# SwiGLU-like gate on one core: load 2 held until tile 1 has landed, the last tile in parts of 2, 3 and 3 rows, one closing wait instruction

## The chip, the core and the metric

The kernel runs on one core of a Trainium2 chip. A core has a matrix engine (TensorE, unused here), VectorE (DVE), ScalarE (ACT), GpSimd (POOL) and SyncE (SP), and 16 DMA engines that move data between the device's memory (HBM) and the on-chip memory (SBUF, 128 partitions). Two instruction streams issue DMAs in this kernel, SP and ACT; each fills a queue of its own (q1 for SP, q10 for ACT in the profile), and both queues are served by the same 16 DMA engines.

The metric is device time in microseconds of one execution. Before the change the median of three runs is 471.4 us (471.35 to 471.65).

## The reference

The input x has 32 x 512 rows of 2048 float32 values. The left half of each row goes through SiLU and is multiplied with the right half; the result has 1024 float32 values a row.

```python
half_dim = x.shape[-1] // 2
x1, x2 = (x[..., :half_dim].copy(), x[..., half_dim:].copy())
silu_x1 = x1 * (1 / (1 + np.exp(-x1)))
return (silu_x1 * x2).astype(np.float32)
```

134.22 MB are read and 67.11 MB written; there is one SiLU and one product per output value.

## The kernel before

The 16384 rows are cut into 16 tiles of 128 partitions x 8 rows (K = 8). A whole tile is 8.4 MB in and 4.2 MB out. In a whole load, each of the 128 partitions takes 8 consecutive rows, which lie together in HBM, so a partition's share is one contiguous piece of 64 KB; its share of a whole store is one piece of 32 KB. There are two input buffers (xt0, xt1) and two output buffers (ot0, ot1), used in turn, and SiLU is written in place into the left half of the input buffer.

The order of the work on each engine is the order in which the program writes it (`tc.manual_schedule()`); an instruction waits for what it reads, and for the readers of what it overwrites.

- Tiles 0 and 1 are loaded in halves of 4 rows, one half by SP and one by ACT (`load_rows`, lines 53 to 54 and 71 to 73). The pieces of these four loads are 32 KB. All four are issued at the start.
- Tile 0 is computed in four parts of 2 rows (`FIRST`), each one SiLU (`silu`, line 58, ScalarE) and one product (`mul`, line 62, VectorE). It is stored by three DMAs from ACT, over every second partition and two sets of every fourth (`OPENING`, line 81). Then SP issues the load of tile 2 (`load(2)`, line 82, which runs line 51). That load overwrites xt0, so it waits for the last product of tile 0.
- For tiles 1 to 14 there is one SiLU, one product, one store from ACT (`store`, line 67) and, up to tile 13, one load of tile i + 2 from SP (line 51). The product waits for the SiLU, and for the store of tile i - 2 to have left its output buffer. The load waits for the product.
- The last tile, 15, is computed in the parts of `LAST`: two of 4 rows. Both SiLUs and products are written first, then the stores (`store`, line 67), so on ScalarE both SiLUs stand ahead of the first store's issue.
- At the end SP gets two empty instructions (`nc.sync.nop()`, line 100). The first waits for the eleven DMAs before the last one, the last SiLU and the last product; the second waits for the last store. After them the program's own end (line 128) waits for what is still open and synchronizes all engines.

`dmas` is the list of all DMAs in the order in which they are written: entries 0 and 1 are the halves of tile 0, entries 2 and 3 those of tile 1, then come the three stores of tile 0, and then load 2.

Of the kernel before, what the change touches and what calls it, by code (L numbers as in the profile page):

```python
# [1 line left out]

# [4 lines left out]


K = 8

FIRST = [(0, 2), (2, 4), (4, 6), (6, 8)]

LAST = [(0, 4), (4, 8)]


OPENING = [slice(0, None, 2), slice(1, None, 4), slice(3, None, 4)]
SYNC = mybir.DependencyInfo(mybir.DependencyClass.Sync, mybir.DependencyReason.DATA)


@with_exitstack  # L20
def kernel(
    ctx: ExitStack,
    tc: tile.TileContext,
    x: bass.AP,
    out: bass.AP,
):
    nc = tc.nc
    P = nc.NUM_PARTITIONS

    x_flat = x.flatten_outer_dims()  # L30
    out_flat = out.flatten_outer_dims()
    num_rows, in_cols = x_flat.shape
    half = in_cols // 2
    dt = x_flat.dtype
    n_tiles = num_rows // (P * K)
    assert n_tiles * P * K == num_rows

    x_view = x_flat.rearrange("(n p k) d -> n p k d", p=P, k=K)
    out_view = out_flat.rearrange("(n p k) d -> n p k d", p=P, k=K)

    in_pool = ctx.enter_context(tc.tile_pool(name="in_pool", bufs=1))
    out_pool = ctx.enter_context(tc.tile_pool(name="out_pool", bufs=1))
    xts = [in_pool.tile([P, K, in_cols], dt, name=f"xt{j}") for j in range(2)]
    ots = [out_pool.tile([P, K, half], dt, name=f"ot{j}") for j in range(2)]

    ctx.enter_context(tc.manual_schedule())

    dmas = []

    def load(i):  # L50
        dmas.append(nc.sync.dma_start(out=xts[i % 2], in_=x_view[i]))

    def load_rows(queue, i, a, b):
        dmas.append(queue.dma_start(out=xts[i][:, a:b], in_=x_view[i][:, a:b]))  # L54

    def silu(i, a, b):
        x1 = xts[i % 2][:, a:b, :half]
        return nc.scalar.activation(out=x1, in_=x1, func=mybir.ActivationFunctionType.Silu)  # L58

    def mul(i, a, b):  # L60
        xt = xts[i % 2]
        return nc.vector.tensor_mul(  # L62
            out=ots[i % 2][:, a:b], in0=xt[:, a:b, :half], in1=xt[:, a:b, half:]
        )

    def store(i, a, b):
        dmas.append(nc.scalar.dma_start(out=out_view[i][:, a:b], in_=ots[i % 2][:, a:b]))

    for i in range(2):
        load_rows(nc.sync, i, 0, K // 2)
        load_rows(nc.scalar, i, K // 2, K)

    for i in range(n_tiles - 1):
        if i == 0:
            for a, b in FIRST:
                silu(0, a, b)
                mul(0, a, b)
            for ps in OPENING:  # L80
                dmas.append(nc.scalar.dma_start(out=out_view[0][ps], in_=ots[0][ps]))
            load(2)
            continue
        silu(i, 0, K)
        mul(i, 0, K)
        store(i, 0, K)
        if i + 2 < n_tiles:
            load(i + 2)

    i = n_tiles - 1  # L90
    for a, b in LAST:
        last_silu = silu(i, a, b)
        last_mul = mul(i, a, b)
    for a, b in LAST:
        store(i, a, b)

    for waited in ([*dmas[-12:-1], last_silu, last_mul], dmas[-1:]):
        seen = nc.sync.nop()  # L100
        for ins in waited:
            tc.add_manual_dep(seen.ins, ins.ins.name, SYNC, reason="the closing waits")


# [1 line left out]
_INS = ['x']  # L106
_OUTS = [((32, 512, 1024), 'float32')]


# [23 lines left out]
```

## Time and profile before

| what | value |
|---|---|
| median of three runs | 471.4 us |
| profiled execution, its own time | 471.62 us |
| its span, first to last instruction | 469.7 us |
| VectorE busy | 139.4 us (30%), 20 products |
| ScalarE busy | 114.1 us (24%), 20 SiLUs and one table load |
| queue q1 (SP: all whole loads, a half of tiles 0 and 1) | 125.83 MB, 62.2% of the DMA engines' time |
| queue q10 (ACT: all stores, a half of tiles 0 and 1) | 75.50 MB, 37.2% |
| HBM read and written | 134.22 MB and 67.11 MB, 429 GB/s over the span |
| whole load, from issue to landing | 42.0 us (median of 14) |
| whole store, from issue to landing | 49.1 us (median of 14) |
| SiLU and product of a whole tile | 7.03 us and 8.69 us |

How to read it: a queue's share is the time that its packets took on the 16 engines, so the two shares together tell how full the DMA engines were. The time from issue to landing includes the time that a DMA's pieces stand behind others on their queue. Each DMA leaves, on every engine that it uses, its data pieces and one short write that reports completion; in the profile these short writes are the packets under 512 B. A window of the DMA view puts a piece's bytes and time into the slice in which the piece starts; where slices are shorter than a piece, the digits show starts, and zeros between them are no idleness by themselves. "Idle before" is what an engine waited for ahead of a group of instructions.

### The profile page before, as it was taken

The page shows a single profiled execution, that of the slowest core. Times are in us where ns is not written, and L with a number is a line of the kernel's source. Part 1 is how long each engine was busy: PE and PEld are TensorE (multiplying, and loading weights), DVE is VectorE, ACT ScalarE, POOL GpSimd, SP SyncE. Part 2 cuts the span into 40 slices and gives each one's busy share as a digit, 9 for nine tenths or more (in the row PEclk, how much of TensorE's full clock was granted, in tenths as well). Part 3 has the DMA queues.
Part 4 walks back from the last instruction along what each step waited for, and adds up shares of the span by engine and source line. Part 5 has one row for each costly group of instructions (what it writes and reads, how often), then busy time and mean ns, then how long its engine had stood idle before and what let it go on. Part 6 is the DMA issues. An engine that isn't in the chain of part 4 may idle for free.

```text
span 469.7 us, 199 instructions
## 1 busy us (share of the span) xinstructions
DVE 139.4 (30%) x20; ACT 114.1 (24%) x21; POOL 0.2 (0%) x4
## 2 busy tenths in 40 slices
DVE  0070704207042070510606115060250702407061
ACT  1053205050140501405023050230503205032060
POOL 0000000000000000000000000000000000000000
DMA  8999998999999999999999999999999899999998
GB/s 357 441 424 430 402 480 374 441 491 402 446 402 486 407 402 446 463 430 402 444 419 477 402 438 410 446 446 421 427 491 435 368 446 491 402 447 402 438 410 357
DMA packets 5073, 201.34 MB, mean 429 GB/s; under 512 B 592, under 2 KB 592, under 8 KB 592
## 3 DMA queue, kind: packets, MB, share of 16 engines
q1 hardware_dynamic: 2304, 125.83, 62.2%
q10 hardware_dynamic: 2768, 75.50, 37.2%
q14 instruction: 1, 0.01, 0.0%
HBM read 134.22 MB, written 67.11 MB: 429 GB/s over the span
## 4 chain that ended last, share of the span: by engine, by line
DMA 80%; DVE 14%; ACT 2%; DVEq 1%; issue 0%; ACTq 0%
DMA out_dram<-ot 62%; DMA xt<-in_x_dram 18%; DVE ot L62 14%; ACT xt L58 2%; DVEq L128 1%; DVEq L62 0%; ACTq L54 0%; ACTq L58 0%
## 5 line engine op out<-in xcount | busy, mean ns | idle before, releaser
L62 DVE TENSOR_TENSOR ot<-xt 128x8192 f32<-128x8192 f32 (+2 forms) x20 | 139.4, 6984 | 320.1 <-ACT xt L58 177.3
L58 ACT ACTIVATE xt<-xt 128x8192 f32<-128x8192 f32 (+2 forms) x20 | 112.8, 5661 | 338.4 <-DMA xt<-in_x_dram 338.4
L58 ACT ACT_TABLE_LOAD x1 | 1.3, 1283 | 1.6 <-PEq L117 1.6
L117 POOL MEMSET const-bfloat16-1.0<- 128x1 bf16 x1 | 0.1, 101 | 0.0
L117 POOL MEMSET const-uint8-127<- 128x1 uint8 x1 | 0.1, 101 | 0.0
L117 POOL MEMSET const-float32-0.0<- 128x1 f32 x1 | 0.1, 98 | 0.2 <-issue 0.2
L117 POOL MEMSET const-float32-1.0<- 128x1 f32 x1 | 0.1, 98 | 0.0
## 6 DMA issues: line engine op xcount, KB each, us to landing
out_dram<-ot ACTq DMA_DIRECT2D x14, 4096.0 KB, 49.1
xt<-in_x_dram ACTq DMA_DIRECT2D x2, 4096.0 KB, 31.7
xt<-in_x_dram SPq DMA_DIRECT2D x2, 4096.0 KB, 31.5
out_dram<-ot ACTq DMA_DIRECT2D x3, 2048.0 KB, 9.2
out_dram<-ot ACTq DMA_DIRECT2D x2, 1024.0 KB, 38.7
xt<-in_x_dram SPq DMA_DIRECT2D x14, 42.0
```

The costliest lines, as they stand in the source:

```text
L58: return nc.scalar.activation(out=x1, in_=x1, func=mybir.ActivationFunctionType.Silu)
L62: return nc.vector.tensor_mul(out=ots[i % 2][:, a:b], in0=xt[:, a:b, :half], in1=xt[:, a:b, half:])
L117: nc = _bacc.Bacc("TRN2", target_bir_lowering=False, num_devices=1)
L128: with _tile.TileContext(nc) as tc:
```

## The change

There are three edits.

1. Load 2 gets two further dependencies: on the two half-loads of tile 1 (`dmas[2:4]`). It is issued only when both have landed, and as before only after the last product of tile 0.
2. `LAST` becomes three parts of 2, 3 and 3 rows. The last tile so has three SiLUs, three products and three stores; as before, all SiLUs and products are written ahead of the stores.
3. One empty SyncE instruction instead of two. It waits for the eleven DMAs before the last one and for the last product. The last SiLU is no longer named (the last product reads its result), and the last store is left to the program's own end.

```diff
-LAST = [(0, 4), (4, 8)]
+LAST = [(0, 2), (2, 5), (5, 8)]
...
-        return nc.scalar.activation(out=x1, in_=x1, func=mybir.ActivationFunctionType.Silu)
+        nc.scalar.activation(out=x1, in_=x1, func=mybir.ActivationFunctionType.Silu)
...
             load(2)
+            for ins in dmas[2:4]:
+                tc.add_manual_dep(dmas[-1].ins, ins.ins.name, SYNC, reason="behind tile 1")
             continue
...
     for a, b in LAST:
-        last_silu = silu(i, a, b)
+        silu(i, a, b)
         last_mul = mul(i, a, b)
     for a, b in LAST:
         store(i, a, b)
...
-    for waited in ([*dmas[-12:-1], last_silu, last_mul], dmas[-1:]):
-        seen = nc.sync.nop()
-        for ins in waited:
-            tc.add_manual_dep(seen.ins, ins.ins.name, SYNC, reason="the closing waits")
+    seen = nc.sync.nop()
+    for ins in [*dmas[-12:-1], last_mul]:
+        tc.add_manual_dep(seen.ins, ins.ins.name, SYNC, reason="the closing waits")
```

## The prediction

> **What bounds the kernel now.** I read the page first, then the table of stretches, then DMA packets in short windows, then the chain of waits and the timeline at both ends.
>
> ```profile
> DVE 139.4 (30%) x20; ACT 114.1 (24%) x21; POOL 0.2 (0%) x4
> q1 hardware_dynamic: 2304, 125.83, 62.2%
> q10 hardware_dynamic: 2768, 75.50, 37.2%
> DMA 80%; DVE 14%; ACT 2%; DVEq 1%; issue 0%; ACTq 0%
> ```
>
> The two DMA queues (q1 is filled by SP, q10 by ACT) hold the 16 DMA engines for 62.2 + 37.2 = 99.4% of the span; VectorE and ScalarE are far from full. The stretches (columns: us, length, VectorE, ScalarE and GpSimd busy, clock, DMA share, GB/s) say where anything is lost:
>
> ```profile
> 22.00:41.00 19.00, 8.90 (x4) 7.31 (x4) 0.00 (x0) 1.00 0.99 426
> 41.00:70.00 29.00, 8.69 (x1) 7.10 (x2) 0.00 (x0) 1.00 1.00 416
> 70.00:99.00 29.00, 8.69 (x1) 7.13 (x2) 0.00 (x0) 1.00 1.00 434
> 446.00:458.00 12.00, 7.29 (x2) 7.12 (x2) 0.00 (x0) 1.00 0.98 423
> 458.00:467.00 9.00, 1.47 (x1) 0.00 (x0) 0.00 (x0) 1.00 1.02 435
> 467.00:469.70 2.70, 0.00 (x0) 0.00 (x0) 0.00 (x0) 1.00 0.24 103
> ```
>
> 434 GB/s is the full rate. The tail keeps it with q10 alone; the last piece ends at 468.36 in the DMA records, 1.3 us before the end. Only 41 to 70, where load 2 starts, runs below the steady rate. A closer window, first at 41:45, then the same place one tile later at 70:74 (40 slices of 0.1 us; a digit stands where pieces start):
>
> ```profile
> DMA  9999999900000000000000000000000000007999
> ```
> ```profile
> DMA  9999990000000000000000007999770000000999
> ```
>
> Pieces of load 2 start at 41.1 to 41.8 and the next pieces only from 44.6: 3.5 us. One tile later a load piece is followed after 2.4 us. In the DMA records the first piece of load 2 takes 3.4 to 3.7 us on all 16 engines, every later load piece 2.418: a stall of 1.09 us per engine. Counted by bytes, 41:70 moved 12.06 MB against 12.58 in 99:128: 0.52 MB, 1.2 us at 434 GB/s. So in the middle there is one stall of about 1.1 us to win and nothing else.
>
> ```profile
> DMA packets 320, 12.06 MB, mean 416 GB/s; under 512 B 80, under 2 KB 80, under 8 KB 80
> ...
> DMA packets 288, 12.58 MB, mean 434 GB/s; under 512 B 32, under 2 KB 32, under 8 KB 32
> ```
>
> The second line also gives the rhythm: 288 packets in 29 us are 128 load pieces of 64 KB, 128 store pieces of 32 KB and 32 completion writes, so per engine 9 turns of q1 and 9 of q10, one against one.
>
> **The change part by part.** (1) Load 2 waits for tile 1. In the chain of waits and the timeline:
>
> ```profile
> 1.17 41.16 DMA xt<-in_x_dram
> 404.83 42.15 DMA xt<-in_x_dram
> 455.13 4.34 DVEq L128
> ```
> ```profile
> 33.64 24.82 SPq L51 DMA_DIRECT2D xt<-in_x_dram  x2
> 33.64 1.84 ACTq L81 DMA_DIRECT2D out_dram<-ot  x3
> 42.35 7.03 ACT L58 ACTIVATE xt<-xt 128x8192 f32<-128x8192 f32 x1 [12.27 <-DMA xt<-in_x_dram]
> ```
>
> Tile 1 lands at 1.17 + 41.16 = 42.33; the issue of load 2 moves from 33.64 to about 42.4. On SP only load 3 stands behind it, and that waits for the product of tile 1 until 58.1, so nothing else is held; POOL issues nothing. From issue to first piece the only row without a backlog is the start: issue at 0.73, first pieces 1.73 to 2.5, so 1.0 to 1.8 us. Load 2's pieces start at 43.4 to 44.2 instead of 41.1. The engines don't idle meanwhile: the three stores of tile 0 (8 pieces per engine, 9.8 us) were issued at 33.64 and stand on q10. They get 2 or 3 turns alone (1.22 us each), and all loads come that much later, all stores sooner. Loads have room: load i+2 is issued 16 us after load i lands, load i+1 ends 29 us after it, so q1 doesn't run dry; nor does q10, since store 1 comes at 58.1 and store 0 lasts beyond 65. Products that now wait for a store (142.8 us in the waits, with Silu ending within 0.1 us of the landing) will wait for Silu instead.
>
> What becomes of the stall is the one large unknown. Bounds: it goes (-1.09), it stays with the first store piece (0), it comes twice (+1.09). Nearest rows: at 21.7 to 22.4 both queues pass to the next DMA at once without a stall (the next pieces follow at the usual pitch), and at 448.4 q10 alone passes from one store to the next without one; at 69 and 98 a load's first piece stands behind a store piece, and is not late. After the change load 2's first piece stands behind store pieces, as in those rows; I take -1.09. Against it: the turn from loads alone to stores happens nowhere else, so those rows can't exclude that it is the store's own start that stalls.
>
> (2) The last tile. At the last load's completion write an engine has 2 pieces of store 13 and 8 of store 14 before it: 10 x 1.22 = 12.2 us, which is 446.0 to 458.2. With 2 or 3 turns given away at the start, store 13 is done and 8 pieces remain (the third turn is a completion write): 9.8 us. By then the first store of the last tile must have come. Rows of the shapes:
>
> ```profile
> L62 DVE TENSOR_TENSOR ot<-xt 128x2048 f32<-128x2048 f32 x4 | 8.9, 2287 | 24.7 <-ACT xt L58 24.7
> L62 DVE TENSOR_TENSOR ot<-xt 128x4096 f32<-128x4096 f32 x2 | 8.8, 4422 | 16.6 <-ACT xt L58 16.6
> L58 ACT ACTIVATE xt<-xt 128x2048 f32<-128x2048 f32 x4 | 7.3, 1897 | 19.8 <-DMA xt<-in_x_dram 19.8
> L58 ACT ACTIVATE xt<-xt 128x4096 f32<-128x4096 f32 x2 | 7.1, 3608 | 21.8 <-DMA xt<-in_x_dram 21.8
> ```
>
> Two Silus take 7.1 us, four take 7.3, so three 7.2. The stores stand behind them on ScalarE: the first issues 0.1 + 7.2 = 7.3 us after the landing (before: 455.16 - 446.98 = 8.2), its product long done (1.9 + 2.3 = 4.2). With 1.0 to 1.8 to the first piece that is 8.3 to 9.1. The cover of 9.8 counts from the completion write, up to 0.5 before the landing on the engine that is last, 1.1 on the first: it ends 8.7 to 9.3 after the landing. So a gap of 0 to 0.4, or none on the late engines; I take +0.15. The last product ends at 1.9 + 2.3 + 3.35 x 2 = 10.9 after the landing instead of 459.5 - 446.98 = 12.5; two stores of work cover that. Smaller pieces: 64, 32 and 16 KB take 2.418, 1.213 and 0.611 us, so each has a fixed 8 ns; 24 instead of 16 pieces per engine cost 0.065.
>
> (3) Closing. The last landing is at 459.50 + 9.2 = 468.7, the end at 469.70. After the landing SP passes steps of about 0.07 us. One empty instruction fewer may remove one or two, and the last store's wait falls to the program's own end: -0.15 to +0.15, taken as -0.05.
>
> Sum: -1.09 + 0.15 + 0.065 - 0.05 = -0.93. The profiled execution took 471.62 (span 469.70, 1.92 around it) and would take 470.7; it lies 0.22 above the median of 471.4, so 470.5 against that median. 0.2%, 0.94 us, is about what a measurement of this kernel can tell from no change: the forecast lies on that edge.
>
> **The rivals.** (a) The stall stays, carried by the first store piece. Then 2 turns at most are given away, no gap comes, and the sum is 0.065 - 0.05: 471.4. For it: the turn from loads to stores has its only row at 41. (b) Slower: the load gives away too many turns. Place: the first store of the last tile. From the fourth turn on each takes 1.22 us of the cover. At four the gap is 0.2 to 1.0, at five 1.4 to 2.2, and 470.5 becomes 472.2; with the stall kept, 473. It decides where the issue of a DMA beside busy queues takes 3 us or more to its first piece. Against it: the 1.0 to 1.8 of the start; for it: no row shows a first piece beside a busy other queue. (c) Pieces are not shared one by one when a queue joins late: load 2 waits for all 8 store pieces, to 51, which takes 8 more turns or 9.8 us from the cover; the tail opens by some 9 us: 479. Against it: the 66.7 to 33.5% shares of q1 and q10 in 99:128 and the one-for-one order at 41. The Trainium skill (DMA: Bandwidth & Descriptors, Queues, rings and completion order) says that an engine drains some 9 to 17 descriptors of one row before it passes to the next, which would be this case; the trace's order of one piece each disagrees.
>
> **How the numbers follow.** Stall gone, tail covered: 0.48, 470.2 to 471.0, six tenths of it beyond 0.2%. (a) 0.35, 471.2 to 471.7, nearly all within 0.2%. (b) 0.15, up to 473, most of it slower. (c) 0.02. The likeliest gives 470.5; the range from 470.1 to 472.2 leaves out the ends of (b), (c) and a little below. Faster 0.48 x 0.6 = 0.29; slower 0.13 of (b), 0.02 of (c), 0.02 of (a) = 0.17; the rest 0.54 is the same.
>
> **What would show it.** Load 2's issue at 42.4 and its first pieces at 43.4 to 45; in 41:45 store pieces every 1.22 us; 41:70 at 434 GB/s. The last load landing 1 to 3 us later than 446.98; the first store of the last tile issued 7.3 us after that, and 434 GB/s from there to the end. Wrong would be: a hole after 41 (a), a hole some 10 us after the last landing (b), load 2's pieces starting only at 51 (c).

## The result and the profile after

The changed kernel takes 472.42 us (median of 17 runs, 472.02 to 472.86) against 471.51 us before (median of 17, 471.05 to 472.44). The ratio is 1.002, with a 95% interval of 1.0012 to 1.0027: 0.9 us slower, where 0.9 us faster was forecast. The profiled execution took 472.85 us; its span is 470.7 us against 469.7.

The page of the changed kernel (busy time, the two queues with their packets, MB and share, and the chain that ended last):

```profile
DVE 139.5 (30%) x21; ACT 114.2 (24%) x22; POOL 0.2 (0%) x4
q1 hardware_dynamic: 2304, 125.83, 62.0%
q10 hardware_dynamic: 2912, 75.50, 37.3%
DMA 72%; DVE 14%; ACT 11%; DVEq 1%; issue 0%; ACTq 0%
```

The bytes are the same and the engines are as busy as before; ScalarE's share of the chain rose from 2% to 11%, because the products on the chain now wait for their SiLU and no longer for a store. The table of stretches of the changed kernel (us, length, VectorE, ScalarE and GpSimd busy, clock, DMA share, GB/s) says where the time went:

```profile
41.00:70.00 29.00, 8.69 (x1) 7.03 (x1) 0.00 (x0) 1.00 0.99 425
70.00:99.00 29.00, 8.69 (x1) 7.03 (x1) 0.00 (x0) 1.00 1.00 434
...
446.00:458.00 12.00, 2.54 (x2) 4.84 (x3) 0.00 (x0) 1.00 0.97 418
458.00:460.80 2.80, 2.80 (x1) 2.38 (x1) 0.00 (x0) 1.00 0.90 375
460.80:462.00 1.20, 1.20 (x2) 0.00 (x0) 0.00 (x0) 1.00 0.14 58
462.00:469.00 7.00, 2.38 (x1) 0.00 (x0) 0.00 (x0) 1.00 1.02 428
```

From 70 on the middle runs at the full 434 GB/s. New is the row 460.80 to 462.00: 58 GB/s, while VectorE is busy all the time. Summed over the DMA records, the 16 engines stand idle there for 1.1 us on average. Before, that part of the tail was full. The timeline of the changed kernel, at the front and in the last tile, and the end of its chain of waits:

```profile
33.65 1.83 ACTq L81 DMA_DIRECT2D out_dram<-ot  x3
43.47 7.03 ACT L58 ACTIVATE xt<-xt 128x8192 f32<-128x8192 f32 x1 [13.38 <-DMA xt<-in_x_dram]
43.61 15.98 SPq L51 DMA_DIRECT2D xt<-in_x_dram  x2
...
453.16 4.56 ACT L58 ACTIVATE xt<-xt 128x2048 f32<-128x2048 f32 x2 [22.09 <-DMA xt<-in_x_dram]
455.10 2.29 DVE L62 TENSOR_TENSOR ot<-xt 128x2048 f32<-128x2048 f32 x1 [15.31 <-ACT xt L58]
457.43 0.34 ACTq L67 DMA_DIRECT2D out_dram<-ot  x1
457.63 2.75 ACT L58 ACTIVATE xt<-xt 128x3072 f32<-128x3072 f32 x1
457.75 6.63 DVE L62 TENSOR_TENSOR ot<-xt 128x3072 f32<-128x3072 f32 x2 [0.36 <-ACT xt L58]
461.15 3.60 ACTq L67 DMA_DIRECT2D out_dram<-ot  x2
```
```profile
410.47 42.60 DMA xt<-in_x_dram
453.08 0.02 issue
453.10 0.02 ACTq L58
453.11 0.04 issue
453.16 4.57 ACT xt L58 x2
457.73 0.02 issue
457.75 3.36 DVE ot L62
461.11 3.27 DVEq L130
```

The last load lands at 453.08 instead of 446.98, 6.1 us later. Its first store is issued at 457.43, and its pieces follow store 14 at 458.3 with hardly a gap. They are 8 pieces of 8 KB per engine, 2.5 us, and on most engines done near 460.85. The second product can't start before the second SiLU ends at 457.7; it ends at 461.11, its store is issued at 461.15, and the first pieces start at 461.99. That is the hole.

The spans add up. The last piece ends at 469.57 instead of 468.36, 1.21 us later; from there to the end of the span it is 1.16 us instead of 1.34. Together 1.0 us.

At the front, the DMA view of the changed kernel, 41:45 in slices of 0.1 us and 43:51 in slices of 0.2 (a digit stands where pieces start):

```profile
DMA  0000008000007999700700007999900700007999
```
```profile
DMA  0099730099703099703099907099700009907079
```

From 42.2 on store pieces start every 1.22 us, as expected. But load 2, issued at 43.6, has its first piece only at 47.2 to 48.6, by engine, after four or five store pieces: 3.6 to 5.0 us after the issue. (The expectations below were written with 6.2 as the upper end; counted by the first piece of each engine it is 5.0.) The engines don't lose the same number of turns, and the last load's reports of completion arrive from 450.0 to 453.1, by engine, where before they arrived from 446.3 to 447.0.

### The profile page after: what moved, and what is told of

The parts are those of the page before. It is cut to its first block, busy times and chain, and to the rows that moved or that the text cites. A ratio compares the mean times of both kernels' runs of the same rounds, so it can differ in the third digit from the quotient of the medians.

```text
span 470.7 us, 202 instructions
## 1 busy us (share of the span) xinstructions
DVE 139.5 (30%) x21; ACT 114.2 (24%) x22; POOL 0.2 (0%) x4
## 4 chain that ended last, share of the span: by engine, by line
DMA 72%; DVE 14%; ACT 11%; DVEq 1%; issue 0%; ACTq 0%
DMA xt<-in_x_dram 72%; DVE ot L62 14%; ACT xt L58 11%; DVEq L130 1%; ACTq L54 0%; ACTq L58 0%
```

## The experiments

Each experiment has its own runs of the kernel before beside it, with medians of 471.44 to 471.51 (the ratios and 95% intervals are those on record; they can differ from the quotient of the two medians by 0.05%). The theory (T) after the result: the wait lets q10 run ahead, which takes away the backlog of stores that covered the computation of the last tile, and the loss is the hole there. The rivals: the loss is made at the front (F), by the small parts (P), or by the closing (C).

### The wait alone

```diff
             load(2)
+            for ins in dmas[2:4]:
+                tc.add_manual_dep(dmas[-1].ins, ins.ins.name, SYNC, reason="behind tile 1")
```

> Load 2 waits for tile 1; the last tile stays in two parts of 4 rows and the closing waits stay as before. Theory T (the loss is a hole in the DMA stream of the last tile, because the wait takes the store backlog away that covered its SiLU and product): the last load lands near 453.1 as in the changed kernel, the first product ends 8.1 us later at 461.2, its first store pieces start near 462.0, store 14 ends near 458.4, so a hole of 3.5 to 3.7 us and about 475.1 us, slower than the changed kernel itself. Rival F (the loss is made at the front, by the later start of load 2 and the engines that fall out of step, and the parts of the last tile do not matter): the same 472.4 as the changed kernel.

475.54 us, ratio 1.0081 (1.0067 to 1.0094): 4.0 us slower than before, and 3.1 slower than the whole change. The stretches of its tail:

```profile
446.00:458.00 12.00, 1.56 (x1) 5.21 (x2) 0.00 (x0) 1.00 0.95 410
458.00:458.90 0.90, 0.90 (x1) 0.90 (x1) 0.00 (x0) 1.00 0.01 0
458.90:461.70 2.80, 2.80 (x2) 1.01 (x1) 0.00 (x0) 1.00 0.00 0
461.70:471.00 9.30, 3.50 (x1) 0.00 (x0) 0.00 (x0) 1.00 1.03 435
```

No data piece starts from about 458 to 461.7. The last load landed at 452.71, the first product of 4 rows was ready at 460.9, its pieces start at 461.74. Theory T holds in place and size: the records have 3.5 us of idle time per engine here, of the 4.0 that were lost. F falls as the main cause of this loss, since the same front gives another time with other parts; some 0.5 us are left for it.

### The parts alone

```diff
-LAST = [(0, 4), (4, 8)]
+LAST = [(0, 2), (2, 5), (5, 8)]
```

> Only the parts of the last tile become 2, 3 and 3 rows. Theory T: the last load lands near 447.0 as before, store 14 lasts to 458.2, the stores of the last tile are issued at 451.3, 455.0 and 458.3, each before its turn, so no hole; 8 more pieces per engine at 8 ns cost 0.065: 471.6 against 471.5 before. Rival P (the smaller parts themselves lose the time, because the first store is too short to cover the second product): slower by 0.9, 472.4.

471.77 us, ratio 1.0001 (0.9993 to 1.001): the same as before. In the last tile the DMA stream has no hole:

```profile
446.00:458.00 12.00, 8.47 (x3) 7.22 (x3) 0.00 (x0) 1.00 0.97 416
458.00:460.80 2.80, 0.36 (x1) 0.00 (x0) 0.00 (x0) 1.00 1.03 436
460.80:462.00 1.20, 0.00 (x0) 0.00 (x0) 0.00 (x0) 1.00 1.01 430
```

The small first store costs nothing while the backlog lasts to 458 and the second store is issued at 455.1. P falls.

### The closing alone

```diff
-    for waited in ([*dmas[-12:-1], last_silu, last_mul], dmas[-1:]):
-        seen = nc.sync.nop()
...
+    seen = nc.sync.nop()
+    for ins in [*dmas[-12:-1], last_mul]:
...
```

> Only the closing waits become one empty instruction. In the changed kernel the end comes 0.78 us after the last landing (469.92 to 470.70), before it came 0.97 after it (468.73 to 469.70). Theory T: 0.1 to 0.2 us faster than before, 471.3. Rival C (the closing holds the loss): slower by about 0.9.

471.30 us, ratio 0.9992 (0.9983 to 1.0002). The interval holds both no change and 0.2% less; slower by 0.9 us is out, so C falls. That it gains 0.1 to 0.2 us is likely and not shown by the times. In the traces, one execution each, the end of the span comes 0.82 us after the last landing, against 0.97 before.

### The whole change with four parts of 2 rows

```diff
-LAST = [(0, 2), (2, 5), (5, 8)]
+LAST = [(0, 2), (2, 4), (4, 6), (6, 8)]
```

(against the changed kernel)

> The changed kernel with the last tile in four parts of 2 rows. The last landing stays near 453.1. Theory T: products end 4.3, 6.5, 8.7 and 10.9 us after the landing, each store is 2.5 us of pieces from 458.4 on (to 460.9, 463.4, 465.9, 468.4), and the second store is issued near 459.6 with its first pieces near 460.5, before 460.9: no hole, and 471.3 to 471.5, within 0.2 of before. Rival F: the loss stays, 472.4.

472.10 us, ratio 1.0012 (1.0004 to 1.0021). The hole is gone:

```profile
458.00:460.80 2.80, 2.80 (x2) 2.25 (x2) 0.00 (x0) 1.00 0.92 386
460.80:462.00 1.20, 1.20 (x2) 0.00 (x0) 0.00 (x0) 1.00 1.04 437
```

The second product ends at 459.4 here, in time. Yet only 0.3 us of the median and 0.7 of the span are won back, not 0.9 to 1.1: the time is still 0.6 above before, which is what rival F asks of a part of the loss. One reason is in the DMA records of the changed kernel: the hole of 1.1 is a mean. In that execution the slowest engine ends its pieces of the first store at 462.07, when the second store's pieces are there, and hardly waits at all: without the hole it would have ended no sooner. In the other profiled execution of the changed kernel (next section) the slowest engine is done at 461.15 and waits 0.8 us. So what the hole costs depends on how late the slowest engine of an execution is; by the medians, 472.10 against 472.42, it is 0.3 us.

### The changed kernel again, and the four parts without the wait

The first of these two is the changed kernel itself, measured again beside the four-part kernel without the wait, on another chip than the experiments above.

> The changed kernel beside the others of this call on the same chip, so that hole, parts and wait are compared under like conditions. Expected 472.4; the hole of about 1.1 us in 460 to 462 of its DMA stream again.

472.54 us, ratio 1.0022 (1.0014 to 1.0031), and 1.07 us of idle time between 460 and 462. Against this median the four parts are worth 0.4 us.

Four parts and the single closing instruction, without the wait:

```diff
-LAST = [(0, 4), (4, 8)]
+LAST = [(0, 2), (2, 4), (4, 6), (6, 8)]
...
-    for waited in ([*dmas[-12:-1], last_silu, last_mul], dmas[-1:]):
-        seen = nc.sync.nop()
...
+    seen = nc.sync.nop()
+    for ins in [*dmas[-12:-1], last_mul]:
...
```

(against the kernel before)

> The kernel with the wait ended at 472.1 with four parts of 2 rows and no hole, still about 0.6 above before. This one has the same four parts and the same single closing instruction, but load 2 does not wait. Theory W (what is left of the loss comes with the wait, in the engines being out of step): 471.3 to 471.5. Rival P (it comes with the many small pieces of the last tile): 472.1.

471.56 us, ratio 0.9999 (0.9991 to 1.0008). So the rest of the loss comes with the wait (W) and not with small pieces. The two intervals touch (1.0004 to 1.0021 with the wait), but the times do not: the slowest of the eleven runs without the wait took 471.85 us, the fastest of the eleven with it 471.94, on two chips on which the kernel before differs by 0.05. By the DMA records the packets of the four-part kernel take 467.45 us per engine with the wait and 467.10 without, and the engines are idle 0.16 us more. Of the 0.35, 0.12 is the stall at the turn from loads to stores (0.91 us without the wait, 1.04 with it), and 0.24 is lateness in single load pieces at 48 to 55, just after load 2 has joined. The engines also end further apart: the last whole store ends at 458.52 on the slowest engine without the wait and at 459.03 with it. Why single pieces are late and engines fall apart is not shown. These are one execution each; the size of this part, 0.3 to 0.6 us, is no better known than that.

### What the stall of 1.1 us at 41 is: an early store

```diff
+    probe = out_pool.tile([P, 128], dt, name="probe")
+    nc.vector.memset(probe, 0.0)
+    nc.scalar.dma_start(out=out_view[0][:, 0, :128], in_=probe)
+
     for i in range(2):
         load_rows(nc.sync, i, 0, K // 2)
```

> The kernel before with a store of 64 KB of zeros into the output of tile 0 put ahead of the two ACT loads (the real store of tile 0 overwrites it later). It tells what the stall of 1.1 us at 41 is. Theory S1 (the cost of the first store of the program on each engine, paid once): the first load piece after tile 1 takes 2.42 us like all others, the stall moves to the start, where it lies in part beside the start of the loads: 470.4 to 471.4. Rival S2 (it belongs to the turn of an engine from loads to whole stores, or to the switch of both queues at once): the stall stays at 41 with 1.0 to 1.1 us, and the time is 471.5 to 471.8.

472.08 us, ratio 1.0018 (1.0007 to 1.0028). The early store has landed by 15.4 us, and the first piece of load 2 is still 0.91 us late on the mean of 16 engines, at 41 to 43. S1 falls. The cost of this kernel has another source: q10 gives one turn to each 512 B piece (they start 1.24 us apart on an engine, beside q1's pieces of 1.21), so the half of tile 0 behind it lands at 32.4 instead of 22.9. Load 2 and the stores are then issued at 38.9 instead of 33.6, and three engines stand idle for 1.4 to 2.0 us until load 2's first piece comes at 43.0 to 43.4.

### Where the delay of load 2 comes from: a finer store of tile 0

```diff
-            for ps in OPENING:
-                dmas.append(nc.scalar.dma_start(out=out_view[0][ps], in_=ots[0][ps]))
+            for r, s in FIRST:
+                store(0, r, s)
```

(against the changed kernel)

> The changed kernel with the store of tile 0 in four DMAs of 2 rows, so in pieces of 8 KB instead of 32. Only the front is read: how long after its issue load 2 gets its first pieces (3.6 to 6.2 us in the changed kernel, beside pieces of 1.22 us). Theory L (an engine has a few store pieces of q10 already in hand when the load arrives, and they go first; the delay is counted in pieces): 1.2 to 2.5 us after the issue. Rival D (the issue itself takes so long while the other queue is busy): 3.6 to 6.2 us again.

Load 2 is issued at 43.23 and its first pieces start at 46.54 to 47.10, 3.3 to 3.9 us later, behind some 14 pieces of 8 KB, of which 10 to 12 start after the issue; its DMA view over 43:51 (slices of 0.2 us) shows the dense small pieces up to 46.8, then the load:

```profile
DMA  9799799798998996999990000000013999000000
```

Neither side is quite right. The delay is not a number of pieces: in the changed kernel 2 to 4 pieces of 32 KB start between the issue and load 2's first piece. It is mostly a time, about 3.3 us (D); but beside 32 KB pieces it is up to 5.0 and spread over 1.4 us, beside 8 KB pieces over 0.6, so a piece in hand comes on top (L). A fixed amount of data that an engine has in hand would look much the same, since 11 pieces of 8 KB and 3 of 32 KB are 88 and 96 KB; no run tells the two apart.

The one run took 474.47 us, and its trace says more about the stall. The store of tile 0 gave one 8 KB piece a turn and lasted so long that the product of tile 2, which needs its output buffer, started only at 91.6. The load behind that product was issued at 100.33, q10 ran out of stores at 100.3 to 100.6, and both queues started anew, load first. The DMA view over 98:106 (slices of 0.2 us; load pieces start at 101.3 to 101.8, the next pieces, of a store, from 105):

```profile
DMA  9900099900000000999000000000000000099333
```

These 16 load pieces take 1.2 to 1.8 us longer than 2.42, 1.43 on the mean, though a whole store had ended on the same engines 0.7 to 1.4 us before. So the stall is not paid once in a program. With 0.9 us of idle time at the same place it makes 2.3 of the 3.0 us that this run lost.

### The stores wait too

```diff
                 dmas.append(nc.scalar.dma_start(out=out_view[0][ps], in_=ots[0][ps]))
+                for ins in dmas[2:4]:
+                    tc.add_manual_dep(dmas[-1].ins, ins.ins.name, SYNC, reason="behind tile 1")
```

(against the changed kernel)

> The changed kernel, in which the three stores of tile 0 wait for tile 1 as well, so that load 2 and store 0 are both issued near 42.4 with both queues empty. It measures two disputed things by themselves. First, the time from the issue of load 2 to its first pieces, 3.6 to 6.2 us in the changed kernel. Theory B (the busy other queue makes it): 1.0 to 1.8 us as at the start. Rival D (the issue of such a load takes this long in any case): over 3 us. Second, the stall of 1.1 us in the last pieces of tile 1. Theory Q (it comes when a store piece stands in line behind loads alone): tile 1 lands near 42.3 at the latest or 1 us sooner than in the changed kernel (43.4), its pieces keep 1.213 us, and the stall shows on the first pieces after 43. Rival E (the end of the opening loads makes it): the last pieces of tile 1 are late again. Time: some 2.5 us without transfer at 42 to 44.5 less the stall, and turns even again so that the tail is covered: 472.5 to 474.

474.86 us, ratio 1.0064 (1.0047 to 1.0081), 0.9 above the range that was expected. Its DMA view at 39:43 and 43:49 (slices of 0.1 and 0.15 us):

```profile
DMA  7770000079979770000000000000000000000000
```
```profile
DMA  0099990000000000000000000009990905099909
```

Load 2 is issued at 42.42 and its first pieces start at 43.37 to 43.83: 1.0 to 1.4 us. So on empty queues the start is as short as at 0.73, and it is the busy other queue that makes it 3.3 to 5.0 (B). The last pieces of tile 1 have their 1.213 us and tile 1 lands at 42.26, 1.2 us sooner than in the changed kernel; the stall is now on the first pieces after 43, which are 1.42 us late (Q). The engines stand still for 2.2 us from 41.2 to 43.5, and at the end their last pieces lie between 470.4 and 472.0, with fifteen of the 16 engines done by 470.9, so one engine is late; why is not known. With even turns the tail is covered: the last load lands at 450.49, and no hole follows.

### Tile 1 from SP alone

```diff
-        load_rows(nc.scalar, i, K // 2, K)
+        load_rows(nc.sync if i else nc.scalar, i, K // 2, K)
```

(against the kernel before)

> The kernel before, with both halves of tile 1 issued by SP, so that q10 is empty from about 22 on and store 0 joins at 34 while q1 is still loading tile 1. Theory Q (the stall belongs to the first whole store pieces that join loads): 16 load pieces near 34 to 36 are 0.9 to 1.1 us longer than 1.213, none at 41, and the time stays at 471.3 to 471.8. Rival V (it belongs to both queues passing to a new DMA at once): no stall anywhere after the start, 470.4 to 470.7, which would beat both kernels.

474.06 us, ratio 1.0055 (1.0043 to 1.0066). The stores are issued at 33.65; q1 streams load pieces, and the first store pieces start at 38.3 to 38.9, 4.6 us after the issue or later:

```profile
DMA  9930989930699965000009933009977007977007
```

(the DMA view over 34:42 in slices of 0.2 us: load pieces to 37, a pause in the starts from 37.2 to 38.2, store pieces from there.) The load pieces before them, at 34 to 39, are longer by 0.83 us on the mean, and at 41 nothing is late. That the stall comes with the first whole store pieces that join a stream of loads (Q) holds; V falls. The expected time was missed by 2.3 us: the stores took turns from 38 on while tile 1 was still being loaded, so the loads fell behind again. This kernel keeps two parts of 4 rows, its last load lands at 451.55, and its tail has 2.6 us of hole, as much as it lost: a second kernel whose loss is a hole in the tail, here without a wait of load 2.

## Why the prediction was wrong

**What bounds the kernel** was right: every run with a full DMA stream lies within 0.2% of before, and the larger losses are holes or stalls in that stream.

**The stall.** The term of -1.09 failed. The change left the stall where it was, on the last pieces of tile 1 instead of the first of load 2 (in the changed kernel 0.61 us on the last q1 piece and 0.51 on the last q10 piece, 1.12 in all). The rows that I took as nearest, other switches of a DMA, don't turn from loads to stores. Rival (a), which the forecast gave 0.35, was the right one here: the turn itself costs it, and the stall followed the stores in the four kernels that moved it. Rival (a) and the turns of rival (b) then came together, for which the prediction named 473 us.

**From issue to first piece.** The term of 1.0 to 1.8 us, taken from the start where the queues are empty, was mis-sized: it measured 3.6 to 5.0. The prediction named this as the open row and put the deciding point of rival (b) at 3 us. It was passed: four or five store pieces instead of 2 or 3, and the last landing 6.1 us later instead of 1 to 3. Rival (b) had the mechanism, with a chance of 0.15, but the wrong place: its gap was to come ahead of the first store of the last tile. (Its gaps of 0.2 to 1.0 and 1.4 to 2.2 us end too low; its own terms, a first piece at 8.3 to 9.1 and a cover of 8.7 to 9.3 less one or two turns, give up to 1.6 and 2.8.) Also the wait itself ended at 43.4 and not at 42.3, because the stall now lay ahead of the landing of tile 1.

**The tail.** That the backlog of stores covers the last tile was right; the step that failed is which part it has to cover. I had the first store held behind all three SiLUs on ScalarE, 7.3 us after the landing; it was issued 4.35 us after it (457.43 - 453.08), as soon as its product was done. So there is no gap ahead of the first store. And I wrote that two stores of work cover the last product, without setting the second product against the end of the first store; with the backlog gone, the first store's 2.5 us are all that covers the second product, which comes 3.7 us after the first (461.15 - 457.43). The hole is 1.1 us on the mean of the engines, the term was 0.15. The two misses act together. By an estimate from the same rows, a last landing only 1 to 3 us later, at 448 to 450, would have had the second store's pieces there 8.9 us after it (461.99 - 453.08), at 457 to 459, with the first store's pieces lasting to 460.7: no hole.

**Loads and stores in the middle** had room, as forecast: no queue ran dry, and the products that waited for stores (142.8 us) wait for SiLU in all cases.

```profile
ACT xt L58 <- DMA xt<-in_x_dram: 344.5, 16, 25.2
DVE ot L62 <- ACT xt L58: 324.9, 17, 24.7
```

(the waits of the changed kernel; the line for stores is gone.)

**The smaller pieces and the closing** were right within what can be measured: 0.065 and -0.05 were forecast; the parts alone measured 1.0001, the closing alone 0.9992.

Put together by the two profiled executions, on the mean of the engines: the stall and the late pieces around it +0.1, the hole +1.1, the pieces +0.07, the end -0.2, which is about the 1.0 us between the spans. But the slowest engine sets the time, and the medians divide the 0.9 us otherwise. The hole is worth 0.3 to 0.4 (four parts against three, with the wait). The other 0.5 to 0.6 stay with the wait when there is no hole; the late pieces and the engines that end further apart are their place, and what makes them is open. Against the forecast of -0.93, the stall that stayed is the largest single miss, 1.1 us. Rival (c) did not occur. The Trainium skill (DMA: Bandwidth & Descriptors, Queues, rings and completion order) says that an engine typically drains 9 to 17 descriptors of one row before it passes to the next. A load that joined here waited, from its issue, for 2 to 4 pieces of 32 KB or 10 to 12 of 8 KB. That is no fixed count of pieces, and after it had joined the two queues took one piece each; how many descriptors make a piece, no run here shows.

## What to carry to other kernels

In a kernel that is bound by its DMA engines, look at the far end when you put a wait at the front: it changes which queue is ahead, and the backlog of stores is what covers the computation of the last tile. The same wait cost 4.0 us with two parts and 0.5 to 0.6 with four. Size the parts of the last tile against what covers each one: the first store's pieces must last until those of the second store can start, here 3.7 us (458.3 to 462.0), and they lasted 2.5. Take the delay from a DMA's issue to its first piece from a row where the other queue is as busy as it will be, not from the empty start.

## What the runs showed of the hardware that was not expected

- A DMA that joins beside a busy other queue gets its first piece 3.3 to 5.0 us after its issue (load 2 beside stores in the changed kernel and with the finer store; 4.6 or more for stores beside loads, with the stall of the next point in it). On empty queues it is 0.85 to 1.8 (0.85 in the tail, 1.0 to 1.4 with the stores held back, 1.0 to 1.8 at the start). The Trainium skill (DMA: Bandwidth & Descriptors, Latency and other measured facts) gives about 0.6 us to the first byte; the runs on empty queues lie above that, and the busy case is far from it. Why the busy case takes so long is not settled.
- The first store pieces that join loads stall each of the 16 engines for 0.8 to 1.4 us on the mean, on the pieces just ahead of them. It followed the stores in all kernels in which they were moved (38 to 42, 41, 34 to 39 and 43 us), a store of 64 KB in pieces of 512 B ahead of it did not take it away, and it came a second time, at 101 us, where the stores had run out and started anew (the finer store). Loads that join stores show no such stall (44 to 48 us in the changed kernel). What makes it is not known.
- ScalarE issues a store as soon as its product is done, although a SiLU that stands ahead of it in the program's order is still to start: in the changed kernel the store at 457.43 comes before the third SiLU at 457.63, and with four parts the store at 457.20 before the fourth SiLU at 458.35.
